# Four first loads reordered, one of them on ScalarE's queue, and a remade instruction list in a hybrid encoder kernel

## The chip, the cores and the metric

The kernel runs on one core of a Trainium2 chip. The metric is the device time of one execution in microseconds (us); a time given for a kernel is the median of its runs. The core has five instruction streams: TensorE (PE in the profile, with its weight loads listed as PEld), VectorE (DVE), ScalarE (ACT), GpSimd (POOL) and SyncE (SP), which here only issues DMAs. Each stream executes strictly in the order in which it was written, and waits on semaphores for the others.

## The reference

Two layers of three blocks each act on x, 256 tokens by 1024, in float32. Layer 0 mixes with a bidirectional mLSTM, layer 1 with windowed attention.

```python
def swiglu(x, w_in, w_out):
    gu = x @ w_in
    g, u = gu[..., :D_FF], gu[..., D_FF:]        # D_FF = 2816
    return (jax.nn.silu(g) * u) @ w_out
...
for l in range(DEPTH):                            # DEPTH = 2
    x = layer_norm(ALPHA * x + 0.5 * swiglu(x, ffn_w_in[l, 0], ffn_w_out[l, 0]), ...)
    y = mlstm_mixer(x, ...) if l % 2 == 0 else window_attention(x, ...)
    x = layer_norm(ALPHA * x + y, ...)
    x = layer_norm(ALPHA * x + 0.5 * swiglu(x, ffn_w_in[l, 1], ffn_w_out[l, 1]), ...)
```

The weights, some 200 MB as moved, come from HBM once; x stays in the core's memory.

## The kernel before

**Arithmetic.** Every float32 factor is split into two numbers of a reduced format, `hi` (a rounded copy, made by ScalarE) and `lo` (what is left, made by VectorE). `mm3` then makes one product out of three matmuls: hi·hi, hi·lo, lo·hi. A weight arrives as a "word" of 128 x 1024 (512 KB) in a raw buffer (`w_raw`, `s_raw`), and `Weights.split` (line 410) turns it into `w_hi` and `w_lo`. In the four feed-forward blocks most of the first product uses Strassen-like combinations of words and of x (`seven`, tiles `S_hir`, `S_lor`), some of them summed by accumulating DMAs that GpSimd issues.

**Stages.** Six stages run one after the other: feed-forward, mLSTM, feed-forward, feed-forward, attention, feed-forward. Tokens are held as two tiles of 128, `x0` and `x1`. Before a matmul can use x or an intermediate, it is turned: TensorE transposes four 128 x 128 pieces into one PSUM bank (a "turn"; `to_xT`, `tr`, `turn`), ScalarE copies the bank to the `hi` tile and VectorE makes the `lo` tile. There are 388 such transposes in the program.

**Order.** The code does not issue instructions; `Program` records them (6678 operations), and `issue` (line 311) sends them out in the order of a written list, `ORDER`, whose entries are steps from one recorded operation to the next. A second written list, `SLOTS`, says which buffer or PSUM bank each tile gets; reusing a buffer creates a wait. Since `issue` makes every call, nearly every instruction of the profile has its line, L320, and is told apart by its tiles.

**The start.** Lines 594 to 601 record the first loads, all on SyncE's queue. `load_x(t, h)` fetches half h (512 columns, 256 KB) of token tile t. The first word of the plan comes in two halves of 256 KB, the others whole:

```python
    load_x(0, 0)
    W.load(plan[0]["word"])
    load_x(1, 0)
    W.load(plan[1]["word"])
    load_x(0, 1)
    load_x(1, 1)
    W.load(plan[2]["word"])
    W.load(plan[3]["word"])
```

TensorE meanwhile transposes the identity matrix (`warm`), turns the first half of x0, multiplies it by the first word, turns the first half of x1, multiplies that by the first word, and goes on to the second word with both token tiles; the second halves of x come after that.

**The end.** `Norm.finish` (line 702) normalises a token tile. For the last stage it works in two halves: two VectorE passes per half (subtract the mean and scale by g; multiply by the reciprocal deviation `rs`, which GpSimd computes, and add b), then a store.

Of the kernel before, what the change touches and what calls it, by code (L numbers as in the profile page):

```python
# [271 lines left out]
    "wt.1": ("1032"),  # L272
    "a_hir.1": ("0101"),
    "a_lor.1": ("1101"),
    "den.1": ("1010"),
    "hst.1": ("1011"),
    "hmv.1": ("1110"),
    "hrs.1": ("0101"),
# [1220 lines left out]
```

## Time and profile before

| | |
|---|---|
| time, median of 3 runs | 933.11 us (930.17 to 934.05) |
| time of the profiled execution | 930.4 us |
| its span, first to last instruction | 928.7 us |
| TensorE busy | 912.4 us, 98% of the span, 4381 matmuls and transposes |
| VectorE, ScalarE, GpSimd busy | 88%, 63%, 15% |
| HBM read | 206.65 MB, 224 GB/s over the span |

The stages end, as the normalisations on VectorE show, near 182, 290, 470, 648, 749 and 921 us. "Busy" for TensorE counts a matmul from its start to a modelled end, and matmuls overlap: a short wait can hide inside a busy stretch, so that the distance between the starts of two matmuls says more than the busy share.

### The profile page before, as it was taken

To read this page: it belongs to the slowest core of one execution; us is meant where nothing else is said; L and a number is where in the kernel's file an instruction comes from. 1 tells how busy PE (TensorE), PEld (TensorE's weight loads), DVE (VectorE), ACT (ScalarE), POOL (GpSimd) and SP (SyncE) were. 2 spreads that over 40 slices of the span, in tenths; PEclk is the share of its full clock that TensorE was granted. 3 is DMA by queue.
4 is the path that set the end of the run, shared out by engine and by line. 5 is a ranking of instruction groups with operands and counts; after the bars stand their busy time and mean duration, and the time that the engine had idled before them with its cause. 6 is when DMAs were issued, how large, how long until landed. Compare 5 with 4: busy or idle time off the path is not lost.

```text
span 928.7 us, 12294 instructions
## 1 busy us (share of the span) xinstructions
PE 912.4 (98%) x4381; PEld 749.5 (81%) x4381; DVE 817.4 (88%) x964; ACT 580.5 (63%) x818; POOL 142.6 (15%) x198
## 2 busy tenths in 40 slices
PE   7999999999999999999999999999999999999996
PEld 6878888889988888888788878888887788888885
DVE  5999979988688999889999989899899799987986
ACT  5758476445764576665737665765589558656660
POOL 0111111110110112111012111111325311202110
PEclk9999999999999999999999999999999999999998
DMA  9899798656552969898867998994842188898961
GB/s 330 259 283 246 240 314 208 230 159 218 180 194 93 335 167 278 262 276 269 239 226 191 315 238 258 282 235 143 282 142 98 46 253 242 250 312 194 300 148 46
DMA packets 100653, 208.50 MB, mean 225 GB/s; under 512 B 6864, under 2 KB 21216, under 8 KB 100592
## 3 DMA queue, kind: packets, MB, share of 16 engines
q1 hardware_dynamic: 82960, 174.09, 53.2%
q0 software_dynamic: 17632, 33.64, 21.5%
q8 instruction: 34, 0.56, 0.2%
q14 instruction: 27, 0.22, 0.1%
HBM read 206.65 MB, written 1.05 MB: 224 GB/s over the span
## 4 chain that ended last, share of the span: by engine, by line
PE 92%; ACT 3%; DVE 2%; DMA 1%; issue 1%; POOL 0%; SPq 0%; POOLq 0%; ACTq 0%
PE p L320 92%; ACT w_hi L320 1%; ACT sc L320 1%; DMA w_raw<-in_ffn_w_in_dram 1%; DMA s_raw<-in_ffn_w_out_dram 1%; DVE pr_lor L320 0%; DVE w_lo L320 0%; DVE x L320 0%; ACT q2r L320 0%; DVE rm L320 0%; DVE o L320 0%; DVE s_raw L320 0%; POOL sm L320 0%; ACT es L320 0%; POOL sc L320 0%
## 5 line engine op out<-in xcount | busy, mean ns | idle before, releaser
L320 ACT CAST w_hi<-s_raw 128x1024 fp32r<-128x1024 f32 x246 | 253.4, 1052 | 101.7 <-PE p L320 62.4
L320 DVE TENSOR_TENSOR w_lo<-s_raw,w_hi 128x1024 fp32r<-128x1024 f32 x246 | 293.8, 1220 | 20.5 <-ACT w_hi L320 15.5
L320 DVE TENSOR_TENSOR w_lo<-w_raw,w_hi 128x1024 fp32r<-128x1024 f32 (+1 forms) x160 | 191.5, 1213 | 30.2 <-ACT w_hi L320 26.5
L320 ACT CAST w_hi<-w_raw 128x1024 fp32r<-128x1024 f32 (+1 forms) x160 | 164.5, 1040 | 78.6 <-PE p L320 35.6
L320 PE MATMUL p<-w_hi,xT_hi 128*128 128x512 f32 x512 | 198.8, 402 | 2.9 <-ACT xT_hi L320 2.9
L320 PE MATMUL p<-w_lo,xT_hi 128*128 128x512 f32 x512 | 198.2, 400 | 0.2 <-DVE w_lo L320 0.2
L320 PE MATMUL p<-w_hi,xT_lo 128*128 128x512 f32 x512 | 197.0, 398 | 0.2
L320 PE MATMUL p<-w_lo,h_hir 128*128 128x512 f32 (+1 forms) x323 | 120.9, 393 | 0.0
L320 PE MATMUL p<-w_hi,h_hir 128*128 128x512 f32 (+1 forms) x323 | 120.7, 393 | 0.0
L320 PE MATMUL p<-w_hi,h_lor 128*128 128x512 f32 (+1 forms) x323 | 119.7, 393 | 0.0
L320 PEld LDWEIGHTS p<-w_hi,xT_hi 128*128 128x128 f32 x512 | 96.4, 189 | 24.2 <-ACT xT_hi L320 3.5
L320 PEld LDWEIGHTS p<-w_hi,xT_lo 128*128 128x128 f32 x512 | 96.6, 189 | 20.5 <-DVE xT_lo L320 1.4
L320 PEld LDWEIGHTS p<-w_lo,xT_hi 128*128 128x128 f32 x512 | 96.4, 189 | 20.2 <-DVE w_lo L320 0.5
L320 POOL DMA_DIRECT2D s_raw<-in_ffn_w_in_dram x43 | 52.1, 1236 | 354.8 <-DVE s_raw L320 111.2
L320 PE MATMUL p<-w_lo,S_hir 128*128 128x512 f32 x256 | 97.0, 390 | 0.4 <-DVE w_lo L320 0.4
L320 PE MATMUL p<-w_hi,S_lor 128*128 128x512 f32 x256 | 97.1, 391 | 0.0
L320 PE MATMUL p<-w_hi,S_hir 128*128 128x512 f32 x256 | 96.6, 392 | 0.5 <-ACT t L320 0.5
L320 PEld LDWEIGHTS p<-w_lo,h_hir 128*128 128x128 f32 x323 | 60.6, 188 | 13.1 <-DVE w_lo L320 0.3
L320 PEld LDWEIGHTS p<-w_hi,h_hir 128*128 128x128 f32 x323 | 60.7, 188 | 12.8 <-ACT h_hir L320 0.8
L320 PEld LDWEIGHTS p<-w_hi,h_lor 128*128 128x128 f32 x323 | 60.7, 188 | 12.3 <-DVE h_lor L320 0.4
L320 ACT CAST h_hir<-p 128x512 fp32r<-128x512 f32 x40 | 23.4, 585 | 56.9 <-PE p L320 56.7
L320 PEld LDWEIGHTS p<-w_hi,S_hir 128*128 128x128 f32 x256 | 48.1, 188 | 11.9 <-ACT t L320 1.9
(195 smaller groups left out, 1245.6 us busy)
## 6 DMA issues: line engine op xcount, KB each, us to landing
s_raw<-in_ffn_w_in_dram SPq DMA_DIRECT2D x102, 512.0 KB, 6.1
s_raw<-in_ffn_w_out_dram SPq DMA_DIRECT2D x59, 512.0 KB, 6.4
w_raw<-in_ffn_w_in_dram SPq DMA_DIRECT2D x57, 512.0 KB, 5.8
s_raw<-in_ffn_w_in_dram POOLq DMA_DIRECT2D x43, 512.0 KB, 6.7
w_raw<-in_ffn_w_out_dram SPq DMA_DIRECT2D x29, 512.0 KB, 6.0
w_raw<-in_ml_w_in_dram SPq DMA_DIRECT2D x24, 512.0 KB, 4.2
w_raw<-in_ffn_w_in_dram POOLq DMA_DIRECT2D x21, 512.0 KB, 7.1
s_raw<-in_ffn_w_in_dram SPq DMA_DIRECT2D x18, 256.0 KB, 4.9
```

Source lines behind the costliest of these rows:

```text
L320: f(*args, **kw)
```

## The change

1. `load_x` sends the first half of x1 (`t > h`, that is t = 1, h = 0) by ScalarE's queue; the other three halves stay with SyncE.
2. The recorded order of the first loads becomes: x1 first half, x0 first half, word 0, word 1, x0 second half, word 2, x1 second half, word 3.
3. `ORDER` and `SLOTS` are replaced as a whole. The same 6678 operations are issued, with the same 388 transposes. Between other matmuls, TensorE's list held its transposes in 242 unbroken groups, 172 of them a single transpose; now it holds them in 123 groups, 33 of them single and 36 of exactly four.

```diff
 ORDER = (
-    "10 -10 9 2 -10 12 1 -12 13 1 -13 14 1 -14 15 1 -15 16 1 -16 17 -16 17 1 -17 18 3 1 1 4 84 -87 1 -6 7 2 116 "
...
 SLOTS = {
-    "raw.0": ("013287459063ab128774a0b3152864971524087532961a40b8926a1054b71a381057"),
+    "raw.0": ("310284657392ab105846a2b0183547691837250843691a72b5639a1057b22a480152"),
...
     def load_x(t, h):
         s_ = slice(h * 512, h * 512 + 512)
-        nc.sync.dma_start(xt[t][:, s_], x[0, t * 128:(t + 1) * 128, s_])
+        (nc.scalar if t > h else nc.sync).dma_start(xt[t][:, s_], x[0, t * 128:(t + 1) * 128, s_])
...
     W = Weights(nc, rooms, words, plan, after)
+    load_x(1, 0)
     load_x(0, 0)
     W.load(plan[0]["word"])
-    load_x(1, 0)
     W.load(plan[1]["word"])
     load_x(0, 1)
+    W.load(plan[2]["word"])
     load_x(1, 1)
-    W.load(plan[2]["word"])
     W.load(plan[3]["word"])
```

Three places show what the new lists move. In the names, a number behind a tile is its buffer, `x_134` is x0 and `x_135` x1.

ScalarE at the very start, before: `w_raw_64` is word 0 (in halves), `w_raw_65` word 1, `p_95` and `p_90` are the banks with the turned first halves of x0 and x1.

```order
L320 ACT_TABLE_LOAD
L320 CAST w_hi_73<-w_raw_64 128x512
L320 CAST xT_hi<-p_95 128x4x128
L320 CAST w_hi_73<-w_raw_64 128x512
L320 CAST w_hi_71<-w_raw_65 128x512 x2
L320 CAST xT_hi<-p_90 128x4x128
```

ScalarE at the same place now: `w_raw_67` is word 0, `w_raw_65` word 1, `p_91` and `p_94` are the two banks.

```order
L314 DMA x_135<-in_x_dram 128x512
L314 ACT_TABLE_LOAD
L314 CAST xT_hi<-p_91 128x4x128
L314 CAST w_hi_71<-w_raw_67 128x512 x2
L314 CAST w_hi_75<-w_raw_65 128x512
L314 CAST xT_hi<-p_94 128x4x128
L314 CAST w_hi_75<-w_raw_65 128x512
```

ScalarE issues a DMA ahead of its table load, and the copy of x1's turned half stands behind one half of word 1 where it stood behind both.

TensorE in the first feed-forward stage, before: `p_93` takes one turn of an intermediate (`t_2`).

```order
L320 MATMUL p_93<-ident,t_2_156 128x128
L320 MATMUL p_91<-w_lo_82,xT_hi 128x512
L320 MATMUL p_90<-w_lo_86,h_hir_1_99 128x512
L320 MATMUL p_95<-w_hi_73,xT_hi 128x512
L320 MATMUL p_93<-ident,t_2_156 128x128
L320 MATMUL p_89<-w_hi_75,h_lor_0_100 128x512
L320 MATMUL p_95<-w_lo_85,xT_hi 128x512
L320 MATMUL p_93<-ident,t_2_156 128x128
L320 MATMUL p_95<-w_hi_73,xT_lo 128x512
L320 MATMUL p_93<-ident,t_2_156 128x128
```

The same turn now (`t_1`, again into `p_93`), up to its third transpose.

```order
L314 MATMUL p_88<-w_hi_70,xT_lo 128x512
L314 MATMUL p_93<-ident,t_1_155 128x128 x3
L314 MATMUL p_95<-w_hi_71,xT_hi 128x512
L314 MATMUL p_92<-w_hi_75,h_lor_1_101 128x512
L314 MATMUL p_91<-w_lo_78,h_hir_1_99 128x512
```

Three of the four transposes stand together where four single ones stood apart.

VectorE in the last normalisation, before: `mv` is mean and variance, `rs` the reciprocal deviation that GpSimd makes.

```order
L320 TENSOR_SCALAR rs_143<-mv_141 128x1
L320 SCALAR_TENSOR_TENSOR x_135<-x_135,mv_141,s_raw_5_131 128x512
L320 SCALAR_TENSOR_TENSOR x_135<-x_135,rs_143,w_raw_64 128x512
L320 SCALAR_TENSOR_TENSOR x_135<-x_135,mv_141,s_raw_5_131 128x512
L320 SCALAR_TENSOR_TENSOR x_135<-x_135,rs_143,w_raw_64 128x512
```

The same now:

```order
L314 BN_AGGR mv_141<-stats_138 128x2
L314 TENSOR_SCALAR rs_142<-mv_141 128x1
L314 SCALAR_TENSOR_TENSOR x_135<-x_135,mv_141,s_raw_0_126 128x512 x2
L314 SCALAR_TENSOR_TENSOR x_135<-x_135,rs_142,s_raw_7_133 128x512 x2
```

The second half's first pass stands ahead of the first half's second pass, the one that needs `rs`.

More of the change, by code (lines that the diff above doesn't have):

```diff
@@ L39 @@
 ORDER = (
[209 rows of a table removed]
[203 rows of a table added]
 )
 SLOTS = {
-    "raw.0": ("013287459063ab128774a0b3152864971524087532961a40b8926a1054b71a381057"),
-    "p": ("7744325206731506124537454743375457543454571365625034571602334670142065174560513274231016436504721047"
-        "5326155054754750457575404507412565364123501474161461741661674477632470437516732406253710275432706523"
-        "4767601710671106716076121037450764235170242060264024646240026"),
+    "raw.0": ("310284657392ab105846a2b0183547691837250843691a72b5639a1057b22a480152"),
@@ L255 @@
+    "p": ("2361465267076413642572050257052727205203204216104257346125643410720315412735704762031032627145603150"
+        "4264317175057055107050171142061751740651736662040264420066204241201267251243267315610234607154062714"
+        "0525265663256632563236371250342507143621515077051105707150177"),
     "h_hir.0": ("10101"),
-    "h_lor.0": ("01010"),
-    "w_hi": ("5370894531758291603421823794501675184623914075826314957082631495708269143506972514793860251479386025"
-        "1473986205147398620514739862051473986512047398065241790298543670512364078951236407895123640785913402"
-        "6784379150628437916205843796025184370962518405176493186205784319620578431962054873196254718309576241"
-        "8309576243180957624318095762481309576182430751869243058639247106258391460725839164072538190467528043"
-        "976056214978"),
@@ L262 @@
-    "w_lo": ("8086513492562891901346926843714235585419360827135046980731264859073216487920853647261905384762198530"
-        "4728593160472859317240863951274086325097318406257029831524670289613487635021498763502417896352704931"
-        "8632094758163209475816320946581732908743156207592413692307584619073258419607328541960725431390216785"
-        "3492016857934201856793402176935802417958230946173825091634768512640397652174369280319465782938541630"
-        "254075286430"),
-    "t.0": ("03054124313205423145140120541"),
@@ L268 @@
-    "stats": ("010000010111"),
-    "mv": ("100010111111"),
-    "rs": ("001101100111"),
-    "raw.1": ("32032032032130213021302130213021"),
[L272 to L275, printed above, removed]
-    "hst.1": ("1011"),
-    "hmv.1": ("1110"),
-    "hrs.1": ("0101"),
-    "h_hir.2": ("1010101010"),
-    "h_lor.2": ("0101010101"),
-    "raw.2": ("96587402371896540a2b98645a7023b175a3904825b17a6390b41a8376954a2083756920b831705b6928314a6b98210347a5"
-        "2107b38641a52097b3a1502869b713432867"),
@@ L283 @@
-    "t.2": ("2451205134235134050144351041514250135042551344523325415422"),
-    "sc.4": ("5105205234215024502140"),
-    "raw.4": ("52025252102543012540"),
-    "rm.4": ("12201120"),
-    "nm.4": ("12022011"),
-    "sm.4": ("21212120"),
-    "es.4": ("22210000"),
-    "pr0_hir.4": ("01010110"),
-    "pr0_lor.4": ("10100100"),
-    "pr1_hir.4": ("10100111"),
-    "pr1_lor.4": ("01010100"),
-    "o.4": ("00110100"),
-    "h_hir.5": ("01010"),
-    "h_lor.5": ("01001"),
-    "raw.5": ("132b32b1970628a43b582613ab7950a84b7069523ba8401769ab87402165902943b5"),
@@ L298 @@
-    "t.5": ("14254034125421204150135143025"),
+    "h_lor.0": ("10010"),
+    "w_hi": ("3759063987516238248506728136740289256013953748250349107285436910723548619024578361259047836125904837"
+        "6129503874612950387614295081734659280716534298017653297690134826075183694207518369420751836940721398"
+        "5642187039564218709365421876903452183765932186304675934218095763421809573642581907632489750613872495"
+        "0163782410956378241059637824015963782041695378426907184685947218936074821569730481625973840162793615"
+        "243261708934"),
@@ new lines @@
+    "w_lo": ("0694569384254036594617051398472830452143692780153976214085373649015823091657382041593678402159368047"
+        "1250897416235089743201569473812065942017236049357412461829305749482153409267918342560714908653170864"
+        "3257834906123578496102537894712753041894293674914765430854193265754819360528479316204591067439201856"
+        "3479201345968701345296780145639287416357920741563425890274910876832910287614592015736402197862340518"
+        "792047126847"),
+    "t.0": ("20315553143105122040201230230"),
@@ new lines @@
+    "stats": ("110100101010"),
+    "mv": ("010011111111"),
+    "rs": ("101101010000"),
+    "raw.1": ("31030310310213023021012301201320"),
+    "wt.1": ("1023"),
+    "a_hir.1": ("1010"),
+    "a_lor.1": ("1010"),
+    "den.1": ("1101"),
+    "hst.1": ("1011"),
+    "hmv.1": ("0010"),
+    "hrs.1": ("0001"),
+    "h_hir.2": ("0100110101"),
+    "h_lor.2": ("1000101001"),
+    "raw.2": ("95684731250476983a1b6a48795312b07952a08619b3457ba039284b676598104ba5761304b1a0536924b1786094213b578a"
+        "21370b46518a23970b81a3276904305b2764"),
@@ new lines @@
+    "t.2": ("1204305412031340301344210350441201354210311452005242345344"),
+    "sc.4": ("1024351350425012354035"),
+    "raw.4": ("05121212150432104215"),
+    "rm.4": ("10211212"),
+    "nm.4": ("00012112"),
+    "sm.4": ("12001202"),
+    "es.4": ("20122102"),
+    "pr0_hir.4": ("10100110"),
+    "pr0_lor.4": ("11010101"),
+    "pr1_hir.4": ("11100011"),
+    "pr1_lor.4": ("00000000"),
+    "o.4": ("01001001"),
+    "h_hir.5": ("01110"),
+    "h_lor.5": ("01101"),
+    "raw.5": ("32b0350217495a86230ba7598361042b8364a08b1327596704a32b5906874b094571"),
@@ L299 @@
+    "t.5": ("00430521330431420453415033415"),
 }
```

411 rows, old and new, of the table ORDER are left out of this document.

## The prediction

> **What bounds the kernel now.** I read the page first, for the chain of work that ended last.
>
> ```profile
> span 928.7 us, 12294 instructions
> ...
> PE 92%; ACT 3%; DVE 2%; DMA 1%; issue 1%; POOL 0%; SPq 0%; POOLq 0%; ACTq 0%
> ```
>
> TensorE holds 92% of the chain: the order of the other engines matters only where TensorE waits for them. The view by stretches says where that is (columns: length, busy time and count of PE, PEld, DVE, ACT, POOL, then granted clock, DMA share, GB/s).
>
> ```profile
> 0.00:25.00 25.00, 20.27 (x84) 15.72 (x85) 13.72 (x19) 15.48 (x21) 0.42 (x5) 0.93 0.92 334
> 25.00:50.00 25.00, 25.00 (x116) 20.67 (x115) 24.49 (x27) 17.39 (x22) 5.03 (x4) 1.00 0.81 230
> ...
> 675.00:735.00 60.00, 57.69 (x348) 47.48 (x347) 51.65 (x97) 49.28 (x141) 25.96 (x50) 1.00 0.30 104
> 735.00:920.00 185.00, 185.00 (x850) 151.30 (x850) 165.03 (x181) 108.89 (x131) 23.36 (x19) 1.00 0.75 216
> ```
>
> TensorE is idle for 4.7 us of the first 25, for 2.3 us of the attention's core (675 to 735), and not at all in the last stage. So there are three places to gain: the start, the attention, and the 8.7 us after TensorE's end at 920. Elsewhere only the length of TensorE's own list counts. In the attention the longest wait, from the waits of that window, is small:
>
> ```profile
> PE p L320 <- POOL sc L320: 0.9, 1, 0.9
> ```
>
> The start, in the timelines of SyncE, ScalarE and TensorE (start, length, what, and in brackets the idle time before it and who ended it):
>
> ```profile
> 2.18 0.43 SPq L320 DMA_DIRECT2D x<-in_x_dram  x1
> 2.66 0.43 SPq L320 DMA_DIRECT2D w_raw<-in_ffn_w_in_dram  x1
> 4.19 0.62 ACT L320 CAST w_hi<-w_raw 128x512 fp32r<-128x512 f32 x1 [2.12 <-DMA w_raw<-in_ffn_w_in_dram]
> 4.74 0.59 ACT L320 CAST xT_hi<-p 128x512 fp32r<-128x512 f32 x1
> 5.79 0.62 ACT L320 CAST w_hi<-w_raw 128x512 fp32r<-128x512 f32 x1 [0.47 <-DMA w_raw<-in_ffn_w_in_dram]
> 9.32 1.14 ACT L320 CAST w_hi<-w_raw 128x512 fp32r<-128x512 f32 x2 [2.91 <-DMA w_raw<-in_ffn_w_in_dram]
> 10.37 0.58 ACT L320 CAST xT_hi<-p 128x512 fp32r<-128x512 f32 x1
> 7.76 0.60 PE L320 MATMUL p<-ident,x 128*128 128x128 f32 x4
> 11.00 0.50 PE L320 MATMUL p<-w_hi,xT_hi 128*128 128x512 f32 x1 [2.64 <-ACT xT_hi L320]
> 11.34 0.41 PE L320 MATMUL p<-w_lo,xT_hi 128*128 128x512 f32 x1
> 11.84 0.79 PE L320 MATMUL p<-w_hi,xT_lo 128*128 128x512 f32 x1
> ...
> 14.56 0.59 PE L320 MATMUL p<-w_hi,xT_lo 128*128 128x512 f32 x1
> 14.99 0.41 PE L320 MATMUL p<-w_hi,xT_hi 128*128 128x512 f32 x1
> 15.23 0.40 PE L320 MATMUL p<-w_lo,xT_hi 128*128 128x512 f32 x1
> ```
>
> TensorE had turned x1's first half by 8.36 (7.76 + 0.60), but the copy to `xT_hi` stood behind both halves of word 1 on ScalarE, and word 1 landed at 9.32. So the wait of 2.64 us is a wait for word 1, through ScalarE's order, and not for x1. It costs a second time: the matmul starts are 0.43 us apart at 14.56 and 0.24 at 14.99. The granted clock explains that:
>
> ```profile
> 4.75:8.17 3.42, 3.12 (x16) 2.00 (x14) 1.99 (x3) 1.19 (x3) 0.00 (x0) 1.00 0.84 264
> 8.17:11.58 3.41, 0.77 (x4) 0.30 (x2) 1.09 (x2) 1.62 (x3) 0.00 (x0) 1.00 1.04 399
> 11.58:14.99 3.41, 3.31 (x8) 2.48 (x8) 2.21 (x4) 2.72 (x4) 0.00 (x0) 0.50 1.05 389
> ```
>
> After a stretch with 0.77 us of work the clock was granted at 0.50 for 3.41 us, which is 1.7 us of work lost; after one with 3.12 us it stayed at 1.00.
>
> **The start, changed.** Word 1's issue moves up by one place on SyncE (from 2.66 to 2.18), since x1's half is ScalarE's. The bytes on the way up to word 1 are the same 1.5 MB, so I leave its landing at 9.32. The bounds: if two queues fill the 16% that the DMA engines were idle in 4.75 to 8.17 (share 0.84), it lands 0.5 us earlier; if the second queue's issue holds up the first's, 0.43 later, the length of one issue. At 9.32 ScalarE casts one half of word 1 (1.14 / 2 = 0.57 us) and then x1's half: TensorE goes on at 11.00 - 0.57 = 10.43. The DMA issue ahead of ScalarE's table load takes about the 0.43 us of SyncE's rows; ScalarE has 2.12 us of idle time before its first cast to hide that.
>
> Sharing has a price in front of that. x1's half (256 KB) now travels beside x0's half, so word 0's halves may come one 256 KB piece later: the first at 5.79 instead of 4.19, the second at about 5.79 + (9.32 - 5.79) / 3 = 6.97 instead of 5.79 (three pieces of 256 KB landed in that stretch). TensorE's work up to x1's turn then slides by up to 1.6 us, to 9.96. What hides it is the idle time up to 10.43, and 0.5 us of it is left; without that cover it would cost the 1.6 us.
>
> The slide helps the clock. In 8.17 to 11.58 TensorE would now work some 1.8 us (8.17 to 9.96, with pauses) and 1.15 us (10.43 to 11.58), between 2.3 and 2.9 us against 0.77 and 3.12 in the rows above: nearer to the row that kept its clock. I take the cold 3.41 us as gone, a gain of 1.7; the other end is 0. The Trainium skill (TensorE: Matmul & The Clock Gate, Part 1: The HAM clock gate) says that the clock follows how busy the array was in a window of about 3.4 us that runs freely and does not begin with the kernel; the three rows agree in length and direction. By that rule the place of the window differs between executions, and this gain could come and go with no change in the kernel.
>
> So TensorE is ahead by 0.57 + 1.7 = 2.3 us at about 17 us. VectorE then limits what is kept: in 25 to 50 us it is busy 24.49 of 25.00, and the pieces it makes first depend on DMAs that keep their times. I keep two thirds, 1.5 us; ends 0 and 2.8 (0.57 + 1.7 + 0.5).
>
> **Transposes in fewer groups.** A single transpose among matmuls, and a group of four:
>
> ```profile
> 428.43 0.39 PE L320 MATMUL p<-w_hi,hc_hir 128*128 128x512 f32 x1
> 428.66 0.27 PE L320 MATMUL p<-ident,t 128*128 128x128 f32 x1
> 428.68 0.47 PE L320 MATMUL p<-w_hi,xT_hi 128*128 128x512 f32 x1
> 429.00 0.39 PE L320 MATMUL p<-w_lo,xT_hi 128*128 128x512 f32 x1
> 613.29 0.40 PE L320 MATMUL p<-w_hi,xT_lo 128*128 128x512 f32 x1
> 613.53 0.60 PE L320 MATMUL p<-ident,t 128*128 128x128 f32 x4
> 613.88 0.48 PE L320 MATMUL p<-w_hi,xT_hi 128*128 128x512 f32 x1
> 614.20 0.40 PE L320 MATMUL p<-w_lo,xT_hi 128*128 128x512 f32 x1
> ```
>
> From the matmul before to the second one behind: 0.57 us with one transpose, 0.91 with four. Two bare steps are 0.46 (a step is 0.23, as from 428.43 to 428.66). One transpose costs 0.11, four cost 0.45, that is 0.11 each: nearly all of it is the transpose itself. With the 0.01 us that the rows resolve, a group's own cost is 0.00 to 0.01 us. Times 119 groups fewer: 0 to 1.2 us; I take 0.7. The move that gives this part of the change its name is worth almost nothing by itself.
>
> **The end.** VectorE's last passes:
>
> ```profile
> 921.55 0.74 DVE L320 SCALAR_TENSOR_TENSOR x<-x,mv,s_raw 128x512 f32<-128x512 f32 x1
> 922.74 0.75 DVE L320 SCALAR_TENSOR_TENSOR x<-x,rs,w_raw 128x512 f32<-128x512 f32 x1 [0.44 <-POOL rs L320]
> 923.41 0.75 DVE L320 SCALAR_TENSOR_TENSOR x<-x,mv,s_raw 128x512 f32<-128x512 f32 x1
> 924.19 0.75 DVE L320 SCALAR_TENSOR_TENSOR x<-x,rs,w_raw 128x512 f32<-128x512 f32 x1
> ```
>
> The wait for `rs` (0.44 us) falls where the second half's first pass now stands. Four passes back to back at 0.67 to 0.78 us a step (the distances of the last three starts) end 0.44 to 0.5 us earlier, and the last store with them. Gain 0.5; the first half's store starts about 0.2 later, ahead of the second half's and so off the end.
>
> **The rest of the remade lists.** Same operations, other order and buffers. In the attention, count on TensorE's list the instructions from the last matmul of a step's scores to the first transpose of its scaled weights (`sc`): over the eight steps 52, 65, 75, 38, 59, 44, 42, 34 before, and 44, 52, 59, 42, 49, 44, 41, 30 now. In that time VectorE, ScalarE and GpSimd must finish a step. The lead shrinks by 48 instructions, 8.0 us at 57.69 / 348 = 0.166 us each. Only one wait for `sc` shows before (0.9 us), so most of that lead was spare; grouped turns also start nearer to their last piece. I take +0.6 us; ends -2.3 (all the idle time of 675 to 735 gone) and +8.0. For the other stages the row of 735 to 920 shows a list with no idle time, and the only reason for a change is the buffers: 0, between -0.5 and +2.
>
> **The sum.** -1.5 - 0.7 - 0.5 + 0.6 = -2.1 us against the profiled execution's own 930.4 (span 928.7 and 1.7 around it): 928.3. That execution is near the low end of the three runs (930.17 to 934.05), so against their median the forecast is 933.1 - 2.1 = 931.0 us.
>
> **The rivals.**
> - *The clock stays cold.* The stretch up to 11.58 is still too empty, or VectorE hands the 1.7 us back by 50 us. For it: 24.49 of 25.00. Against: TensorE's work in the stretch at least triples. Then the start gives 0.5 and the sum is -1.1: 932.0.
> - *Sharing costs what it moves.* x0's half and word 0 come late by the full 1.6 us and word 1 is not early, so that TensorE reaches x1's turn after the copy could have started, and the early stretch (4.75 to 8.17) is the empty one. Then the cold clock moves forward instead of going, and the start is worth -0.57 + 0.57 = 0: sum -0.6, 932.5. The Trainium skill (DMA: Bandwidth & Descriptors, Issuing engines are not separate DMA queues) states this side of it: DMAs started by different engines run on the same 16 DMA engines and interleave, so a second queue saves only issue time. No run shown here has two hardware queues at once; the sum of this rival stands without it.
> - *Slower: the attention's leads were needed.* The place is the step from scores to `sc`, the price is 0.166 us per instruction of lead lost, and it decides once more than 2.7 us of the 8.0 turn into waiting. For it: the wait of 0.9 us shows one step with no spare lead, and that step's lead shrinks from 65 to 52. Against: one wait in eight steps. All of it: 933.1 + (-2.7 + 8.0) = 938.4.
> - *The change does not do what it says*: excluded for the groups (242 to 123) and the loads, both stand in the lists.
>
> **The numbers.** Forecast 0.50, cold clock 0.17, sharing 0.13, attention 0.20. Half a percent (4.7 us) is about what a measurement of this kernel can tell from no change: faster means below 928.4, slower above 937.8. The forecast's own ends (start 2.8, groups 1.2, end 0.5, attention -2.3) reach 933.1 - 6.8 = 926.3, and the median itself moves by 1 or 2 us between triples, so the forecast gives faster nearly half of its 0.50; the two middle rivals lie within; the slower one is beyond 937.8 in three cases of four. That makes faster 0.24, same 0.61, slower 0.15. The range takes in the lower end and most of the slower rival: 926.5 to 937.5.
>
> **What would show it.** In the changed profile: TensorE's wait before the first matmul with x1 ends near 10.4 and is under 1.5 us; the granted clock is 1.00 from 11.58 to 14.99; the transposes of the second halves of x start near 15 instead of 17; VectorE's four last passes stand back to back; from 735 to 920 TensorE stays busy throughout. The forecast is wrong if a wait for `sc`, `pr` or `q2r` of over 1 us shows in more than one step of the attention, if TensorE waits for weights anywhere behind 50 us, or if the cold stretch is still there at full length.

## The result, and the profile after

The changed kernel takes 923.07 us (median of six executions, 922.33 to 923.82); the kernel before took 930.84 beside it (930.05 to 934.05, six). The ratio is 0.9909 with a 95% interval of 0.9892 to 0.9926: faster by 0.9%, some 7.8 us, where 2.1 us were forecast. The time lies below the forecast's range (926.5 to 937.5). The profiled execution took 922.74 us.

From the page, span and chain:

```profile
span 921.0 us, 12305 instructions
...
PE 95%; DVE 2%; ACT 1%; DMA 1%; issue 0%; POOL 0%; DVEq 0%; ACTq 0%; SPq 0%; POOLq 0%
```

By stretches (columns as before; the last two rows are the attention's core and the last stage, 7 us earlier than before):

```profile
0.00:25.00 25.00, 21.54 (x96) 16.71 (x97) 16.57 (x22) 16.49 (x22) 0.42 (x5) 1.00 0.93 338
25.00:50.00 25.00, 25.00 (x116) 20.65 (x115) 24.14 (x26) 19.25 (x25) 5.04 (x4) 1.00 0.98 266
8.17:11.58 3.41, 2.73 (x13) 1.80 (x13) 1.98 (x3) 2.50 (x5) 0.00 (x0) 1.00 1.02 383
11.58:14.99 3.41, 3.41 (x20) 2.84 (x19) 2.78 (x3) 1.64 (x2) 0.00 (x0) 1.00 1.05 390
668.00:728.00 60.00, 56.99 (x345) 46.29 (x343) 52.01 (x98) 49.65 (x142) 25.79 (x51) 1.00 0.32 110
728.00:913.00 185.00, 185.00 (x853) 153.05 (x852) 165.17 (x180) 109.21 (x131) 23.28 (x19) 1.00 0.76 219
```

The cold stretch is gone, the attention's core has 3.0 us of idle time where it had 2.3, and the last stage is fully busy as before, with 853 matmuls in 185 us instead of 850: a first sign that "busy" hides something.

The start, ScalarE and then TensorE:

```profile
0.79 0.41 ACTq L314 DMA_DIRECT2D x<-in_x_dram  x1
8.01 0.62 ACT L314 CAST w_hi<-w_raw 128x512 fp32r<-128x512 f32 x1 [0.70 <-DMA w_raw<-in_ffn_w_in_dram]
9.30 0.59 ACT L314 CAST xT_hi<-p 128x512 fp32r<-128x512 f32 x1 [0.67 <-PE p L314]
9.94 0.50 PE L314 MATMUL p<-w_hi,xT_hi 128*128 128x512 f32 x1 [0.68 <-ACT xT_hi L314]
```

Word 1 is there at 8.0 us, not at 9.3. The copy for x1 no longer waits for it but for TensorE's own turn, and TensorE goes on at 9.94 after a wait of 0.68 us (2.64 before).

VectorE's last passes, now back to back:

```profile
914.74 1.41 DVE L314 SCALAR_TENSOR_TENSOR x<-x,mv,s_raw 128x512 f32<-128x512 f32 x2
916.06 1.41 DVE L314 SCALAR_TENSOR_TENSOR x<-x,rs,s_raw 128x512 f32<-128x512 f32 x2
```

Where the 7.7 us between the two spans (928.7 and 921.0) lie, busy shares can't say. So I add up, over neighbouring instructions on TensorE, the distance of their starts beyond what such a pair takes when nothing waits (0.227 us between two 512-wide matmuls, 0.109 between two transposes, and so on for each pair of shapes). I call that lost time; a wait that the view of waits counts as 0.0 is in it. One such wait, before:

```profile
458.93 0.57 ACT L320 CAST h_hir<-p 128x512 fp32r<-128x512 f32 x1
459.16 0.40 PE L320 MATMUL p<-w_hi,h_lor 128*128 128x512 f32 x1
459.56 0.50 PE L320 MATMUL p<-w_hi,h_hir 128*128 128x512 f32 x1
```

The second matmul needs what ScalarE finished at 459.50, and starts 0.40 us after its neighbour where 0.227 would do. No idle time is shown, since the neighbour counts as busy up to 459.56.

| place (us) | lost before | lost after | difference |
|---|---|---|---|
| start, 0 to 25 | 8.31 | 5.68 | -2.6 |
| 25 to 182 | 1.18 | 0.42 | -0.8 |
| 182 to 290 | 1.38 | 0.61 | -0.8 |
| 290 to 470 | 1.03 | 0.41 | -0.6 |
| 470 to 648 | 1.42 | 0.24 | -1.2 |
| attention, 648 to 749 | 6.58 | 7.41 | +0.8 |
| 749 to the last matmul | 0.65 | 0.30 | -0.4 |
| transposes: groups' own cost | | | -1.3 |
| from the last matmul's start to the end | 8.71 | 7.87 | -0.8 |

The row of the groups is the rest: the last matmul starts 6.8 us earlier (919.98, 913.16), 5.5 of that is lost time. The five stages outside start and attention lost 5.7 us and now lose 2.0. That is the largest entry, and the forecast had 0 for it. Distances that are over 0.03 us too long, as waits are, make 2.0 of this 3.7 us (2.4 before, 0.4 after). The rest are steps that differ by less, most of them by under 0.01 us and at matmuls that wait for no semaphore; what makes these longer is not shown.

### The profile page after: what moved, and what is told of

It reads as the page before. It is cut to its first block, busy times and chain, and to the rows that moved or that the text cites. A ratio compares the mean times of both kernels' runs of the same rounds, so it can differ in the third digit from the quotient of the medians.

```text
span 921.0 us, 12305 instructions
## 1 busy us (share of the span) xinstructions
PE 907.0 (98%) x4381; PEld 753.3 (82%) x4381; DVE 818.0 (89%) x964; ACT 580.7 (63%) x818; POOL 142.5 (15%) x198
## 4 chain that ended last, share of the span: by engine, by line
PE 95%; DVE 2%; ACT 1%; DMA 1%; issue 0%; POOL 0%; DVEq 0%; ACTq 0%; SPq 0%; POOLq 0%
PE p L314 95%; DMA w_raw<-in_at_w_out_dram 1%; ACT sc L314 1%; DVE rm L314 1%; DMA x<-in_x_dram 0%; DVE pr_lor L314 0%; DVE x L314 0%; ACT xT_hi L314 0%; ACT pr_hir L314 0%; DVE q2r L314 0%; POOL sc L314 0%; ACT q2r L314 0%; POOL sm L314 0%; DVE nm L314 0%; DVE o L314 0%
## 5 line engine op out<-in xcount | busy, mean ns | idle before, releaser
L314 ACT CAST w_hi<-s_raw 128x1024 fp32r<-128x1024 f32 x243 | 249.6, 1052 | 96.7 <-PE p L314 60.5
L314 DVE TENSOR_TENSOR w_lo<-s_raw,w_hi 128x1024 fp32r<-128x1024 f32 x243 | 289.5, 1219 | 17.3 <-ACT w_hi L314 15.7
L314 ACT CAST w_hi<-w_raw 128x1024 fp32r<-128x1024 f32 (+1 forms) x163 | 168.1, 1042 | 82.2 <-PE p L314 41.4
L314 DVE TENSOR_TENSOR w_lo<-w_raw,w_hi 128x1024 fp32r<-128x1024 f32 (+1 forms) x163 | 194.9, 1210 | 22.1 <-ACT w_hi L314 15.7
L314 PE MATMUL p<-w_lo,h_hir 128*128 128x512 f32 (+1 forms) x323 | 117.8, 389 | 0.0
L314 POOL DMA_DIRECT2D w_raw<-in_ffn_w_in_dram x23 | 28.9, 1274 | 196.2 <-DVE s_raw L314 74.5
```

The source lines that it names most:

```text
L314: f(*args, **kw)
```

## The experiments

All were built from the two kernels; "lists" are what `ORDER` makes of them. The table gives medians, with the ratio to the kernel before that ran beside them. That kernel took 931.13 us beside e1 to e4, 930.58 beside e5 to e8, 929.86 beside e9 to e11, 930.91 beside e12 to e14 and 931.39 beside e15, so runs of different groups compare better by their ratios, which come from all executions and not from the two medians.

| run | what it is | median (range), us | ratio, 95% |
|---|---|---|---|
| e1_loads | before + new loads | 928.74 (927.90-930.98) | 0.9974 (0.9960-0.9989) |
| e2_act | before + ScalarE's order at the start | 929.55 (927.90-932.61) | 0.9985 (0.9967-1.0003) |
| e3_start | before + both | 929.73 (927.36-931.78) | 0.9989 (0.9972-1.0006) |
| e4_group | before + grouped turns | 929.22 (926.47-931.19) | 0.9973 (0.9960-0.9985) |
| e5_all | before + all named parts | 929.10 (925.13-930.40) | 0.9971 (0.9953-0.9989) |
| e6_oldloads | changed, old loads | 922.76 (922.27-923.91) | 0.9911 (0.9891-0.9931) |
| e7_warm | before + work in the first wait | 930.73 (928.07-933.38) | 1.0001 (0.9986-1.0017) |
| e8_agroup | changed + more grouping | 922.75 (922.43-923.11) | 0.9910 (0.9888-0.9933) |
| e9_lead | e5_all + leads on TensorE | 924.13 (922.52-926.86) | 0.9932 (0.9911-0.9954) |
| e10_alead | e8_agroup + leads | 922.03 (921.58-922.52) | 0.9909 (0.9886-0.9931) |
| e11_best | e10_alead + later DMA issue | 921.73 (921.56-922.01) | 0.9905 (0.9878-0.9931) |
| e12_copy | e5_all + four copies moved | 926.50 (925.11-927.39) | 0.9946 (0.9925-0.9966) |
| e13_leadcopy | e9_lead + the same | 923.78 (922.98-925.14) | 0.9920 (0.9902-0.9939) |
| e14_lead3 | e5_all + leads in 290 to 470 | 925.96 (924.66-929.43) | 0.9946 (0.9927-0.9966) |
| e15_oneq | changed, one queue | 923.63 (922.31-925.71) | 0.9921 (0.9896-0.9946) |

### The named parts on the kernel before: e1 to e5

e1_loads is the diff of the change without its lists:

```diff
-        nc.sync.dma_start(xt[t][:, s_], x[0, ...
+        (nc.scalar if t > h else nc.sync).dma_start(xt[t][:, s_], x[0, ...
+    load_x(1, 0)
     load_x(0, 0)
...
-    load_x(1, 0)
```

> The kernel before, with only the loads of the change: x1's first half by ScalarE's queue ahead of everything, the other loads in the new order; all lists as before, so the copy of x1's turned half still stands behind both halves of word 1 on ScalarE. Theory A (the early DMA rate is what changed: with two queues word 1 lands near 8.0 us, where it was 9.30): TensorE goes on with x1 near 9.9 us instead of 11.0, the clock stays at 1.00, and the time falls by 2.0 to 2.6 us, all of it kept at 50 us and at the end. Theory B (as the prediction had it: word 1's landing depends on the bytes ahead of it and stays at 9.3): TensorE goes on at 11.0, the cold stretch stays, and the time changes by less than 0.5 us.

Word 1 landed at 7.75 us, TensorE went on with x1 at 9.73 and its last matmul started 1.75 us earlier than in the kernel before (918.23). The start lost 5.46 us instead of 8.31; 1.1 us of that gain was lost again later in this execution, most of it at 859.7 us, where TensorE waited for a copy to `t` (0.74 us lost). The median fell by 0.26%, 2.4 us.

e2_act moves one cast on ScalarE (and VectorE's passes with it):

```diff
 w_hi <- word 1, second half
-w_hi <- word 1, first half
 xT_hi <- x1's turned half
+w_hi <- word 1, first half
```

> The kernel before, with only ScalarE's order at the start: the copy of x1's turned half stands between the two halves of word 1 (VectorE's three passes in the order that goes with it); loads as before, word 1 at 9.30. TensorE goes on at 10.4 instead of 11.0. If that is enough work in the stretch up to 11.58 to keep the clock, the time falls by 2.3 us, and by 1.5 us if VectorE hands a third back; if the clock still falls to 0.50 for 3.41 us, it falls by 0.6 us.

TensorE went on at 9.73, since word 1 happened to land at 8.56 here, and the clock stayed warm. The median is 0.15% lower, an interval that holds no change.

e3_start is both.

> The kernel before with both: the new loads and ScalarE's new order at the start, all else as before. If a gain at the start is kept in full (TensorE's list is the bound from there on), TensorE's last matmul starts 2.6 to 2.9 us earlier than in the kernel before and the time falls by as much; if VectorE, busy 24.49 of 25 us in 25 to 50, hands back a third, by 1.7 to 1.9 us, and waits of TensorE for a low part show between 20 and 50 us.

Neither: the start lost 5.82 us, 2.5 less than before, and 25 to 50 us lost 0.17 us: VectorE hands nothing back. But at 415.1 us TensorE waited for 1.87 us where the kernel before had not waited at all, and the last matmul started only 0.5 us earlier. ScalarE and TensorE at that place:

```profile
415.39 1.04 ACT L320 CAST w_hi<-w_raw 128x1024 fp32r<-128x1024 f32 x1 [1.07 <-DMA w_raw<-in_ffn_w_in_dram]
416.34 1.07 ACT L320 COPY t<-p 128x512 f32<-128x512 f32 x2
416.98 0.50 PE L320 MATMUL p<-w_hi,S_hir 128*128 128x512 f32 x1 [1.87 <-ACT t L320]
```

A weight that an accumulating DMA sums up landed late (issued at 403.53, landed at 415.31; 405.99 and 413.88 in the kernel before). ScalarE stood at its cast, the copy that frees a bank stood behind the cast, and TensorE waited for the bank.

e4_group: for each of 206 transposes,

```diff
-transpose p_93 <- t
 matmul ...
 matmul ...
+transpose p_93 <- t
 transpose p_93 <- t
```

> The kernel before with only its turns grouped: each transpose but the last of a turn is moved down TensorE's list to stand right in front of the next one of its turn, 206 moved, 94 groups where there were 242; nothing else is moved, so no copy of a turn comes later than before for that reason. By the many rows of the two traces (a single transpose between matmuls costs 0.119 us, four together 0.443 to 0.451) a group has a cost of its own of 0.011 us: 148 groups fewer save 1.6 us, and the waits in front of early transposes in the attention (up to 0.9 us) may go as well, 1.6 to 3 us in all. By the prediction's 0.006 us a group: 0.9 us. If later transposes hold the source buffers and make ScalarE late, the time rises, and TensorE's waits for t or sc show it.

The last matmul started 3.1 us earlier (916.87): 1.56 us less lost time (about 1.5 of it at the start, where the clock stayed at full speed), and 1.55 us for 148 groups, 0.0105 us each, as the many rows say. The other surprise is the clock. By stretches, with the same wait at the start (2.79 us; 2.64 in the kernel before):

```profile
8.17:11.58 3.41, 0.62 (x2) 0.30 (x2) 1.13 (x2) 1.62 (x3) 0.00 (x0) 1.00 1.04 399
11.58:14.99 3.41, 3.30 (x15) 2.65 (x15) 2.48 (x4) 2.77 (x4) 0.00 (x0) 1.00 1.05 389
```

TensorE worked 0.62 us in the first stretch, less than the 0.77 before, and kept its clock. But these stretches are those of the trace of before, where the granted clock changed at 4.75, 11.58 and 14.99 us: 6.83 and 3.41 us apart, two and one times 3.413. Here it reached full speed at 6.41 us and kept it for 914.77 us, 268 times 3.413, so that the stretches to look at begin at 6.41:

```profile
6.41:9.82 3.41, 1.75 (x10) 1.18 (x8) 0.51 (x1) 0.54 (x2) 0.00 (x0) 1.00 0.96 357
9.82:13.24 3.42, 2.17 (x8) 1.52 (x9) 2.06 (x4) 2.33 (x5) 0.00 (x0) 1.00 1.05 401
```

The same wait is now shared by two stretches, each with over 1.7 us of work. Two traces show no more than this, but they fit a cold stretch that comes only in executions in which one stretch lies over most of the wait.

e5_all has the loads, ScalarE's order, the groups and, at the end:

```diff
 rs <- mv, first half
+x <- x, mv, g, second half
 x <- x, rs, b, first half
-x <- x, mv, g, second half
```

> The kernel before with every part of the change that can be named by itself: the new loads, ScalarE's order at the start, the turns grouped (94 groups), and the last normalisation's second-half pass moved ahead of the pass that waits for rs. Buffers and all other order stay as before. Theory C (the named parts are the gain; the rest of the remade lists does nothing, as the prediction had it): start 2.5, groups 1.6, end 0.9, so the time comes to within 1 us of the changed kernel, near 923 to 924 us. Theory D (the remade order also takes away small waits of TensorE for pieces that come just in time, and those waits differ from execution to execution): it stays 2 to 4 us above the changed kernel, near 925 to 927 us, and its executions spread over 3 us or more where those of the changed kernel spread over 1.5.

929.10 us: all the named parts together are worth 1.5 us in the median, 2.7 us (0.29%) by the ratio. Its ten executions fall into two groups, 925.1 to 926.0 and 929.1 to 930.4; the profiled one is of the lower group, at 925.95. In that one the parts are worth what they should be (the end 8.71 to 8.08), but the stages outside start and attention still lose 5.4 us. Theory C falls. Theory D has the spread right, but not the size: the median is 6.0 us above the changed kernel's.

### What carries the start: e6, e7, e15

e6_oldloads puts the loads of the kernel before into the changed kernel (the diff of e1 backwards).

> The changed kernel with the old loads (all on SyncE's queue, in the old order); all lists as changed, ScalarE's new order at the start included. Word 1 lands between 8.6 and 9.3 instead of 7.98, TensorE goes on with x1 at 9.7 to 10.4 instead of 9.94. If the start is kept to the end in either direction, the time is 0 to 0.7 us above the changed kernel (923 to 923.8 us), so that the loads are a small part of the gain and ScalarE's order is enough. If the loads carry the start's gain, it is 2 us or more above it (925 us or more), with the clock at 0.50 for 3.4 us.

922.76 us, the changed kernel's time. The loads, the first thing that the change names, can't be told from nothing once the lists are remade. (The profiled execution, 923.91, went on with x1 at 10.46 us and lost 0.96 us at 412.6.)

e7_warm, in `issue`:

```diff
         for i in order:
+            if i == 51:
+                f, args, kw = self.ops[29]
+                for _ in range(22):
+                    f(self.ops[51][1][0][:, 0:128], *args[1:], **kw)
             f, args, kw = self.ops[i]
```

> The kernel before with 22 more transposes of the identity matrix on TensorE between the turn of x1's first half and the first matmul with it (into a bank that this matmul starts anew): about 2.4 us of work in a wait of 2.6 us. Loads and all lists as before. If the cold 3.41 us after the wait come from the wait itself, the granted clock is 1.00 from there on in every execution and the time falls by 1.5 to 1.7 us. If they come only in some executions, by where the clock's window falls (the grouped kernel kept its clock with the same wait), the median falls by 0.5 to 1 us and the fastest execution stays where the fastest of the kernel before is, near 928.6 us.

The median did not move (ratio 1.0001), although the fill did its work: in the profiled execution TensorE was busy for 3.22 us from 8.17 to 11.58 and the clock stayed at 1.00. Nor does the cold stretch look rare. The mean granted clock of the execution in which the profile of before shows it was 0.995; 35 of the 82 executions of the kernel before that ran beside the experiments had 0.995 or less, and none of e7_warm's ten had (0.996 to 0.998). Those 35 took 931.5 us on average, the 22 with 0.997 or more 929.4; and still e7_warm is no shorter than the kernel before. So what the fill saves at the start is lost again later in most executions; no trace here shows where. The 1.7 us of the forecast are a price that one execution showed, and not a gain of the median.

e15_oneq has the changed kernel's order of loads with `nc.sync` for all four halves.

> The changed kernel with x1's first half on SyncE's queue, ahead of the others: the new order of the loads, but one queue. Word 1 landed at 9.30, 9.26 and 8.56 us with the old loads (one queue) and at 7.98, 7.75 and 8.05 with the new ones (two queues). If the second queue makes the early transfers themselves faster, word 1 lands near 9 here, as with the old loads. If the bytes ahead of it and the issue time are all, it lands 0.4 to 0.5 us after the 8.0 of two queues, near 8.4. The time of the execution: that of the changed kernel within 0.5 us (922.5 to 923.6) in both cases, since the old loads cost nothing to be told in e6_oldloads.

Word 1 landed at 8.25 us, 0.27 after the changed kernel's, with its issue 0.48 later (2.66, 2.18). In the five profiles with the old loads it landed at 8.56 to 9.36, in the eleven with the new order and two queues at 7.5 to 8.2. One execution decides little, but it stands nearer to the second group: the order of the loads (both first halves of x ahead of word 0) accounts for most of the early landing, and the second queue saved an issue. That agrees with the Trainium skill (DMA: Bandwidth & Descriptors, Issuing engines are not separate DMA queues), by which a second queue saves issue time alone. In the same trace the clock warmed late: matmul starts were still 0.43 us apart at 8.46 to 8.89, 0.23 at the same place in the changed kernel. The time, 923.63 us (ratio 0.9921; 0.9909 for two queues), is just above what was expected, and the two intervals overlap.

```profile
8.46 0.63 PE L314 MATMUL p<-w_hi,xT_lo 128*128 128x512 f32 x1
8.89 0.63 PE L314 MATMUL p<-w_hi,xT_hi 128*128 128x512 f32 x1
9.31 0.46 PE L314 MATMUL p<-w_lo,xT_hi 128*128 128x512 f32 x1
9.61 0.40 PE L314 MATMUL p<-w_hi,xT_lo 128*128 128x512 f32 x1
```

### What carries the gain: leads on TensorE's list, e8 to e11

In a trace I took, for each operation of VectorE or ScalarE that makes a piece for TensorE or copies out a bank that TensorE fills next, the time from its end to the start of the first matmul or transpose that needs it. Outside start and attention there are some 1250 such hand-overs. Under 0.3 us, where TensorE has to wait or all but, are 65 in the kernel before (42 of VectorE, 23 of ScalarE), 49 in e5_all, and 21 in the changed kernel. e9_lead changes TensorE's list and nothing else, at 162 places, like this:

```diff
+matmul, independent, its pieces long ready
 matmul, its last piece ready under 0.6 us ago
-matmul, independent, its pieces long ready
```

> The kernel of e5_all (the kernel before with all named parts) with one thing more: TensorE's list outside the attention gets leads. Wherever e5_all's trace shows a matmul or a group of transposes that starts less than 0.6 us after the last piece it needs was finished by another engine, a later, independent matmul whose pieces are long ready is moved in front of it; 162 matmuls are moved so, the groups stay 94, all other engines' lists and all buffers stay as in e5_all. Theory D (just-in-time hand-overs cost TensorE small waits in every execution, and larger ones in some): TensorE's lost time outside start and attention falls from 5.4 us to about 2, the profiled execution ends 2.5 to 3.5 us earlier than that of e5_all (925.95), and the median comes from 929.1 to between 923 and 926 us. Theory F (it is the remade buffers or the order on the other engines that count): no change, 928 to 930 us.

10 hand-overs under 0.3 us are left, and the median falls from 929.10 to 924.13 us. That overstates it, since e5_all's median lies in the upper of its two groups: by the ratios (0.9971, 0.9932) it is 3.6 us. Buffers and the other engines' lists are those of e5_all, so theory F falls as the main cause; of the 2.1 us that are left to the changed kernel (0.9909) it may hold a part. The profiled execution ends 2.2 us earlier, less than expected, and the five stages still lose some 3.5 us, not 2. The steady waits went: 25 to 182 lost 0.52 us (1.26 in e5_all), 749 to the end 0.16 (1.25). One place got worse in the profiled execution, the one of e3_start, with 1.48 us lost:

```profile
412.33 1.04 ACT L318 CAST w_hi<-w_raw 128x1024 fp32r<-128x1024 f32 x1 [1.07 <-DMA w_raw<-in_ffn_w_in_dram]
413.29 1.07 ACT L318 COPY t<-p 128x512 f32<-128x512 f32 x2
413.92 0.50 PE L318 MATMUL p<-w_hi,S_hir 128*128 128x512 f32 x1 [1.31 <-ACT t L318]
```

The same cure on the changed kernel, first with more grouping (the edit of e4), then with leads:

> The changed kernel with its turns grouped all the way: 111 transposes moved down to the next one of their turn, 81 groups where there are 123; nothing else. At 0.011 us a group TensorE's last matmul starts 0.45 us earlier and the time is 922.4 to 922.6 us; at nothing a group it is 923. A piece that is kept longer for a later transpose could make ScalarE wait for its buffer: then a wait of TensorE for t, sc or pr shows, and the time is above 923.

The last matmul started 0.29 us earlier, where 0.45 were expected, and the median is 922.75, above the 922.4 to 922.6: too little for the times to tell from nothing.

> The kernel of e8_agroup (the changed kernel with 81 groups) with the same treatment of TensorE's list, the attention included: 134 matmuls moved up in front of a matmul or group that started less than 0.6 us after its last piece was ready. Theory D: TensorE's lost time outside the start falls by some 1 to 2 us (in the attention it is 7.6 us there, of which the moves can reach a part), and the time comes to 921 to 922 us. If what is left is no matter of leads, it stays at 922.5 to 923.

922.03 us, at the upper end of what was expected, and outside start and attention 1.24 us are still lost (2.01 in e8_agroup). But the ratio, 0.9909, is that of e8_agroup (0.9910) and of the changed kernel, so the time does not show a gain. The attention did not get better (7.79 us; 7.56); why leads do not help there, no run shows.

e11_best moves one DMA in the list:

```diff
-DMA x1, first half
 ACT_TABLE_LOAD
+DMA x1, first half
```

> The kernel of e10_alead with the issue of x1's first half moved behind the table load on ScalarE (from 0.79 us to about 2.5 us), so that x0's half and word 0 have the DMA engines to themselves at first. x0's half lands near 3.5 us instead of 4.07, word 0's halves 0.5 us earlier, x1's half is still there before TensorE asks for it at 8.4. If the start is kept, 0.3 to 0.6 us less than e10_alead; if x1's half comes late, TensorE waits for it near 8 us and the time rises by up to 1 us.

The edit did not do what it says:

```profile
0.79 1.28 ACT L313 ACT_TABLE_LOAD   x1 [0.79 <-PEq L1479]
0.82 0.39 ACTq L313 DMA_DIRECT2D x<-in_x_dram  x1
```

The issue did not wait for the table load and came at 0.82; x0's half landed at 4.24. What the edit gained is that the table load began at 0.79 instead of 1.23, with nobody waiting for it. 921.73 us (3 hand-overs under 0.3 us) is still the shortest median of the study: its four executions (921.56 to 922.01) all lie below the changed kernel's six, as three of e10_alead's four do. But the kernel before was shorter beside them too (929.86 us, 930.84 beside the changed kernel), and the ratios (0.9905, 0.9909) do not tell the two apart.

### One place that differs between executions: e12 to e14

e12_copy moves four copies on ScalarE, near 413 us these two:

```diff
+t <- p_7
+t <- p_0
 w_hi <- weight summed up by the accumulating DMA
-t <- p_0
-t <- p_7
```

> The kernel of e5_all (the kernel before with all named parts) with ScalarE's list changed at three places and nothing else: near 50, 413 and 858 us, copies of a full bank to t (one, two and one) stand ahead of the cast of a weight in front of which ScalarE waits or works while the bank is full. The executions of e5_all fall into two groups, 925.1 to 926.0 and 929.1 to 930.4. Theory G (what varies is the landing of the accumulated weight at 410 to 415 us: when it is late, ScalarE stands at its cast, the banks behind it stay full and TensorE waits, 2.03 us in e3_start and 1.48 in e9_lead): the upper group goes, the median comes to 924.5 to 926. Theory H (the two groups come from elsewhere, or from many places): the two groups stay, the median is 928 to 929, lower by 0.5 to 1 for the waits at 50 and 858.

The upper group is gone: all six executions lie between 925.1 and 927.4, where six of e5_all's ten lay above 929. The median, 926.50, is 0.5 above what theory G gave. So half or more of the distance from e5_all to e9_lead (2.6 of 5.0 us in the medians, 2.3 of 3.6 by the ratios) goes with these four copies. Two of the four stand near 50 and 858 us, so that this run alone does not single out the place near 413; nor does its profiled execution (927.39 us, the longest of the six), in which the weight landed early, at 411.95.

> The kernel of e9_lead (leads on TensorE's list) with the same four copies ahead of their casts. e9_lead's executions run from 922.5 to 926.9. Theory G: the wait of 1.48 us at 412 goes and the executions stay within 922 to 923.5, so that the order of before, with its own buffers and the named parts, reaches the changed kernel. Theory H: the median stays near 924 and the spread at 3 us or more.

The median, 923.78, is only 0.35 lower than e9_lead's, and the upper end falls from 926.9 to 925.1: theory G's direction at a smaller size. The trace shows the mechanism itself, because the weight came late here too (issued at 401.89, landed at 413.50, 11.6 us as in e3_start and e9_lead):

```profile
412.41 1.05 ACT L318 COPY t<-p 128x512 f32<-128x512 f32 x2
413.52 1.05 ACT L318 CAST w_hi<-w_raw 128x1024 fp32r<-128x1024 f32 x1
413.52 0.50 PE L318 MATMUL p<-w_hi,S_hir 128*128 128x512 f32 x1
```

The copies went ahead, and the matmul that had waited for 1.31 us in e9_lead follows its neighbour (413.19) at 0.33 us.

> The kernel of e5_all with leads on TensorE's list only between 290 and 470 us (35 of the 162 matmuls moved in e9_lead). If the 5 us between the medians of e5_all and e9_lead are the sum of many small waits in all stages, this gives 290 to 470's share of the steady part (0.9 us in e5_all) and the median falls by about 1 us, to 928. If they are mostly the one place at 410 to 415 us, the upper group of executions goes with these 35 moves alone and the median comes to 924.5 to 926.

925.96: 35 matmuls moved in this one stage take 3.1 us off (2.3 by the ratios), of which the steady part could be 0.9 at most; in the profiled execution, of the lower group like that of e5_all, the stage lost no less than there (1.3 us, 0.9). One of seven executions (929.43) still lies in the upper group. Its mean granted clock was 0.995, 0.997 or 0.998 in the other six, so it may be long for another reason.

## Why the prediction was wrong

The step that failed is "For the other stages the row of 735 to 920 shows a list with no idle time, and the only reason for a change is the buffers: 0, between -0.5 and +2". Two things were wrong with it. First, a busy row of TensorE does not show that nothing waits: matmuls overlap (0.39 us long, 0.227 us from start to start), a wait of 0.17 us, as at 459 us, leaves no idle time, and the five stages lost 5.66 us in small pieces, 2.4 us of it in distances over 0.03 us too long (two waits at 52.8 and 542.8 us, 0.65 and 0.53 us, the rest below 0.3). Only the stage from 749 on, the one that I looked at, lost little (0.65). Second, order on TensorE's list is a reason for a change, and I took it for one in the attention alone, where I counted leads; e9_lead shows that leads outside it, with the old buffers, are worth 3.6 us by the ratios (5.0 in the medians). In the pair of profiled executions the step is 3.7 of the 5.6 us that the sum was short of (7.7 measured, 2.1 forecast). The place near 413 us has no part in that: the profiled execution of before lost nothing there.

The other steps, in the forecast's order:

- *Start, -1.5.* It gave -2.6 in the pair of traces. "I leave its landing at 9.32" was wrong (7.98), because the order of the loads counts beside the bytes; the sharing cost about half of what was said (x0's half 0.63 us later, word 0 0.8 to 0.9, where 1.2 to 1.6 were allowed), and the idle time hid it. "VectorE limits what is kept" did not happen: 25 to 50 us lost 0.06 us. One place that takes a gain of the start back is the one near 413, as e3_start shows. In the medians the start is worth 2.4 us (e1_loads) to nothing (e6_oldloads).
- *Clock.* It stayed at 1.00, as said, with 2.73 us of work in the stretch (2.3 to 2.9 forecast). But the price was not the kernel's: e4_group kept its clock with the wait, and e7_warm, which filled the wait and in no execution had so low a mean clock, gained nothing in time. The sentence behind the Trainium skill's rule, that this gain could come and go, was the better forecast, and I still entered the 1.7 us.
- *Groups, -0.7.* 1.3 measured. The two rows resolved 0.01 us and the term was 0.011 x 119; the size came out a tenth above the upper bound. I took a middle value where the median over the many rows (0.119 us for a single transpose, 0.446 for four: 0.109 a transpose, 0.010 a group) would have set it. "Worth almost nothing by itself" was too strong.
- *End, -0.5.* -0.84 in the change; -0.63 by the swap alone (e5_all).
- *Attention, +0.6.* +0.8: the size was right, the place only in part. The lead that was counted ends at `sc`, and the waits for `sc` did not grow (0.9 us before, 0.8 now, with ScalarE's); those for `pr`, one step behind, went from 0.3 to 1.8 us. None is over 1 us. For `pr` before, and then `pr` and `sc` now (total, times, longest):

```profile
PE p L320 <- DVE pr_lor L320: 0.3, 1, 0.3
```

```profile
PE p L314 <- DVE pr_lor L314: 1.1, 3, 0.7
PE p L314 <- ACT pr_hir L314: 0.7, 1, 0.7
PE p L314 <- POOL sc L314: 0.6, 1, 0.6
PE p L314 <- ACT sc L314: 0.2, 1, 0.2
```

- *The rivals.* The cold clock and the price of sharing did not come about, and of the 8 us of lead in the attention under 1 was needed.

The signs named ahead all came (9.94 and 0.68 us for x1's first matmul, x's second halves turned at 14.4, four passes back to back, no wait for weights that the view of waits lists behind 50 us), and the forecast was wrong all the same: I had named no sign for the stages that I took for settled.

What stays open: no execution of e5_all's upper group was profiled, so that its 4 us are laid at the place near 413 by the two cures (e12_copy, e14_lead3) and by the 2.0 and 1.5 us lost there in e3_start and e9_lead, not by its own trace; these are at most half of the 4. Where the gain of a kept clock goes in e7_warm is open too. And e13_leadcopy is 0.7 us above the changed kernel (1.0 by the ratios), for which the buffers and the other engines' lists were not told apart.

## What to carry to other kernels

Where one pipelined engine is the bound, don't read its list's health from its busy share: add up the distances of its starts beyond the bare ones, stage by stage, and count how many of its inputs are finished less than 0.3 us ahead of use. The lists with few such hand-overs were the shorter ones here, though not in strict order: 65 for the kernel before, 49 for 0.9971 of its time (e5_all), 21 for 0.9909 (the changed kernel), 10 for 0.9932 (e9_lead), 3 for 0.9905 (e11_best). And don't let a copy that frees a bank stand in an in-order queue behind an instruction that waits for a transfer.

## What the runs showed of the hardware

- The granted clock reached full speed at 4.75 us in the trace of before, at 5.42 in that after, and between 5.1 and 9.4 in the other fifteen, though TensorE started on the same transposes at 1.45 or 1.46 us in all. The Trainium skill (TensorE: Matmul & The Clock Gate, Part 1: The HAM clock gate) says that the window runs freely; the spread here is wider than the half microsecond either way that it gives.
- In all seventeen traces the full clock lasted whole multiples of 3.413 us, 2 to 269 of them, from a beginning that differed between executions. A wait of 2.6 us that one such stretch covered was followed by 3.41 us at half clock; one of 2.8 us that two stretches shared was not.
- A DMA that ScalarE issues behind its table load in program order goes out while the load runs (0.82 us, in a load from 0.79 to 2.07).
- The same accumulating DMA took 7.9 us from issue to landing in the kernel before and 8.1 to 11.8 in the ten profiled variants that keep its order of DMAs: a spread of nearly 4 us at a place where the DMA engines' share was 0.9 to 1.1.
